# Recurrence rebuilt: 64x64 quarter tiles per head in place of zero-padded 128x128 products, and the triangular inverse by three steps from 8x8 blocks

## The chip, the cores and the metric

One core of one Trainium2 chip. The time is device microseconds of one execution of the whole program, the median of several runs; a profiled execution gives the trace. Engines: PE (matrix products, with weight loads, PEld), DVE (VectorE), ACT (ScalarE), POOL (GpSimd), SP (issues transfers).

## The reference

Two layers over 512 latent and 256 context tokens of 1024 features. Each has attention beside an RWKV-7 mixer, an output projection, and a mixture of single-neuron experts. The part that matters is the mixer's scan: 8 heads of 64 in two directions, the latent scan starting from the last context state, and the second layer needing no context output.

```python
def step(state, inp):
    r_t, w_t, k_t, v_t, kk_t, b_t = inp
    s_kk = jnp.einsum('bhij,bhj->bhi', state, kk_t)
    state = state * w_t[:, :, None, :] - s_kk[..., None] * b_t[:, :, None, :] + v_t[..., None] * k_t[:, :, None, :]
    y = jnp.einsum('bhij,bhj->bhi', state, r_t) if emit else None
    return state, y
```

## The kernel before

Per layer the program runs the projections with attention, the features of the mixer, the recurrence (`rwkv`, L692), and a tail (output projection, experts). The features leave k, b, v, r and the log decays in DRAM by chunks of 64 tokens (`FD`). `rwkv` walks 12 chunks, 4 of context and 8 latent, both directions at once. A head in a direction is one unit: 16 units of a 64x64 state. The heads are cut into two halves (`hf`); a tile of a half holds four blocks u, each with two heads, one in partitions 0 to 63 and one in 64 to 127.

To treat two heads in one product, one operand is padded: `zb` (L698) holds kh, bh, vz and zp as 128x128 blocks with zeros off the two diagonal quarters. `each` (L708) issues four products of 128x128 per half.

Five stages, each for both halves:
- A (L715): loads, exponentials of the decays (Ex, En), the scaled keys and receptances KR, and kh, bh, vz into the padded tiles (kh by POOL).
- B (L759): GB = bh by KR and GK = kh by KR, evacuated with a mask on DVE (L764, L770); kh, bh, vz transposed on PE, copied by ACT.
- C (L782): the inverse of the unit triangular 64x64 matrix in GB, begun with its 16x16 diagonal blocks: blocks gathered into D, 16 shuffles (L801) that spread their rows, 15 steps of forward substitution, two small DVE operations each (L810, L811), and X, the block diagonal (L815).
- D (L823): X grown to 32 and to 64 by two levels: a transpose (L833), q (a masked GB, by POOL through L146), two products (L839, L845), an addition to X on DVE (L846).
- E (L856): the state. zt = GK part plus H part (L860, L867), transposed to Zs (L876), Us = X by Zs (L887), the new state H by kn, bn, Vb, Us on DVE in four pieces (L897, L900, L907), the output added into zt (L919) and to Y (L928, L930).

`merge` (L136) weaves the stages: in iteration m it issues E of chunk m-2, D of m-1, B and C of m, A of m+1 and the loads of m+2, each list spread over a part of the iteration, and `outputs` (L946) of finished chunk pairs. A scheduler then orders the instructions of each engine by priority and dependence; each engine runs its own in that order. In PSUM there are four `ga` and two `ch` tiles, and one `zt` per half.

Of the kernel before, what the change touches and what calls it, by code (L numbers as in the profile page):

```python
# [21 lines left out]
D = 1024  # L22
# [15 lines left out]
def make_consts():  # L38
# [9 lines left out]
    cols["m16"] = ((p % 64)[:, None] // 16 == np.arange(4)[None])  # L48
    cols["eye16"] = (p[:, None] % 16 == np.arange(16)[None])
    cols["x16"] = (p[:, None] // 16 == np.arange(8)[None])  # L50
    P, Q = p[:, None], p[None, :]
    q1f = (P // 32 == Q // 32) & (P // 16 < Q // 16)
    q2f = (P // 64 == Q // 64) & (P // 32 < Q // 32)
    cols["q1"], cols["q2"] = q1f, q2f
# [30 lines left out]
RB = 6  # L85
# [17 lines left out]
def body(ctx: ExitStack, tc: tile.TileContext, I: dict, out: bass.AP):  # L103
# [588 lines left out]
    def rwkv(L, PT, cat, FD, need_ctx, ro, rl):  # L692
# [3 lines left out]
        rw = es.enter_context(tc.tile_pool(name=f"rw{l}", bufs=1))  # L696
# [8 lines left out]
        def bank(nm="ga", nb_=4):  # L705
            return rps.tile([128, 4, 128], F32, name=nm, bufs=nb_)

        def each(dst, f):  # L708
            for u in range(4):
                f(dst[:, u, :], u)  # L710

        def t4(nm, n=2, w=128):
            return (ra if nm in ("Ex", "En", "etot", "KR", "GB") else rw).tile([128, 4, w], F32, name=nm, bufs=n)

        def stage_a(ss):  # L715
            def load(s):
                fd = FD[s["st"], s["hf"]]
                NCH, n = TOK[s["st"]] // C, s["n"]
                fal = s["fal"] = rl.tile([128, 2, 3, 2, C], F32, name="fal", bufs=4)
                fbl = s["fbl"] = rl.tile([128, 3, 4, C], F32, name="fbl", bufs=4)  # L720
                for pp in range(2):
                    for d in range(2):
                        SP.dma_start(fal[:, d, :, pp, :],
                                     fd["a"][NCH - 1 - n if d else n, pp].rearrange("p (f t) -> p f t", t=C))
                    SP.dma_start(fbl[:, :, pp::2, :], fd["b"][n, pp].rearrange("p (f d t) -> p f d t", d=2, t=C))

            def dv(s, f, d, ps=slice(None)):
                t = s["fal"][ps, d, f]
                return t[:, :, ::-1] if d else t

            def a1(s):
                Ex = s["Ex"] = t4("Ex", 2, 65)
                En = s["En"] = t4("En", 2, 64)
                V.memset(Ex[:, :, 0:1], 1.0)
                A.activation(Ex[:, :, 1:65], s["fbl"][:, 2], AF.Exp, scale=-EXPC)
                A.activation(En, s["fbl"][:, 2], AF.Exp, scale=EXPC)
                s["etot"] = t4("etot", 8, 1)
                V.tensor_copy(s["etot"], Ex[:, :, 64:65])

            def a2(s):  # L740
                KR, Ex = t4("KR", RB), s["Ex"]
                s["KR"] = KR
                for d in range(2):
                    u = slice(2 * d, 2 * d + 2)
                    V.tensor_tensor(KR[:, u, 0:64], dv(s, 1, d), Ex[:, u, 0:64], op=mul)
                    V.tensor_tensor(KR[:, u, 64:128], dv(s, 0, d), Ex[:, u, 1:65], op=mul)

            def a3(s):
                for h in range(2):
# [3 lines left out]
                    for d in range(2):  # L753
                        A.copy(zb["vz", s["hf"]][hp, 2 * d:2 * d + 2, 64 * h:64 * h + 64], dv(s, 2, d, hp))
# [1004 lines left out]
```

## Time and profile before

| | us |
|---|---|
| median of 3 runs (4962.43 to 4966.59) | 4963.79 |
| the profiled execution, its own time | 4962.0 |
| its span on the trace | 4960.2 |
| PE busy | 4557.3 (92%) |
| DVE busy | 3918.9 (79%) |
| ACT busy | 2124.4 (43%) |
| POOL busy | 1581.4 (32%) |

The page gives means over the whole span. A stage is read by cutting the span: the recurrence of layer 0 lies near 447 to 855 us, that of layer 1 near 3186 to 3575. A product of f32 operands stands as two MATMUL records, a transpose as one. A record's duration includes a tail in the pipeline, so back-to-back records overlap, and the busy time of many by their count is their pace.

### The profile page before, as it was taken

How to read it: one execution, taken by the hardware profiler on the slowest of the kernel's cores; microseconds unless marked ns; L12 is line 12 of the kernel's file. 1: busy time of each engine (PE TensorE's matmuls, PEld its weight loads, DVE VectorE, ACT ScalarE, POOL GpSimd, SP SyncE). 2: the span in 40 equal slices, each digit the busy share in tenths (PEclk: the TensorE clock that was granted, in tenths of full speed). 3: DMA queues.
4: the chain of work that ended last, by engine and by line, in shares of the span. 5: the costliest groups of instructions: out<-in, count | busy, mean ns of one | idle time of the engine just before them, and what ended most of it. 6: DMA issues, size and time to landing. Idle time of an engine off the chain costs nothing. (4 is left out here: it accounts for less than half of the span.)

```text
span 4960.2 us, 73310 instructions
## 1 busy us (share of the span) xinstructions
PE 4557.3 (92%) x25291; PEld 3870.9 (78%) x25291; DVE 3918.9 (79%) x9256; ACT 2124.4 (43%) x3951; POOL 1581.4 (32%) x1560
## 2 busy tenths in 40 slices
PE   7998899886999999989999989889998999999999
PEld 5664898775777887767777777489877998889998
DVE  2468996699998888877788656799678986888886
ACT  3355554434775232222222235555444773333332
POOL 0212332343222345545455231333222101234441
PEclk8998999998999999999999999999999999999999
DMA  6656221644768999988899532722153768999996
GB/s 232 252 173 179 58 54 32 235 133 135 258 239 305 356 326 325 328 287 298 298 324 328 199 123 79 210 62 50 52 178 108 266 244 304 354 330 331 327 331 214
DMA packets 613733, 1105.96 MB, mean 223 GB/s; under 512 B 219056, under 2 KB 394864, under 8 KB 603632
## 3 DMA queue, kind: packets, MB, share of 16 engines
q1 hardware_dynamic: 502768, 698.57, 42.3%
q0 software_dynamic: 110592, 402.70, 22.7%
q8 instruction: 200, 3.28, 0.3%
q14 instruction: 173, 1.42, 0.1%
HBM read 960.38 MB, written 140.74 MB: 222 GB/s over the span
## 5 line engine op out<-in xcount | busy, mean ns | idle before, releaser
L1263 POOL DMA_INDIRECT u<-in_u,eidx x384 | 479.7, 1249 | 1171.8 <-DVE u L1275 833.8
L159 PE MATMUL u_ps<-phi,uhi 128*128 128x512 f32 (+1 forms) x2048 | 767.4, 375 | 62.3 <-ACT ga L1454 45.5
L159 PE MATMUL u_ps<-phi,ulo 128*128 128x512 f32 (+1 forms) x2048 | 758.9, 371 | 34.2 <-DVE ulo L1449 34.1
L159 PE MATMUL u_ps<-plo,uhi 128*128 128x512 f32 (+1 forms) x2048 | 756.1, 369 | 0.0
L1263 POOL DMA_INDIRECT u<-in_v,eidx x384 | 516.6, 1345 | 521.7 <-DVE gacc L1288 444.0
L1448 ACT CAST uhi<-raw 128x1024 fp32r<-128x1024 f32 x256 | 268.5, 1050 | 917.8 <-PE u_ps L159 574.5
L159 PE MATMUL pa<-vhi,whi 128*128 128x512 f32 x1536 | 601.1, 391 | 7.5 <-ACT whi L150 7.5
L159 PE MATMUL pa<-vhi,wlo 128*128 128x512 f32 x1536 | 603.0, 393 | 0.0
L159 PE MATMUL pa<-vlo,whi 128*128 128x512 f32 x1536 | 602.7, 392 | 0.0
L1288 DVE SCALAR_TENSOR_TENSOR gacc<-u,gw,gacc 128x1024 f32<-128x1024 f32 x381 | 488.4, 1282 | 98.3 <-DMA u<-in_v,eidx 94.7
L1275 DVE SCALAR_TENSOR_TENSOR u<-u,gh 128x1024 f32<-128x1024 f32 x384 | 468.0, 1228 | 114.8 <-DMA u<-in_u,eidx 107.3
L159 PEld LDWEIGHTS u_ps<-phi,uhi 128*128 128x128 f32 x2048 | 393.4, 192 | 117.6 <-ACT ga L1454 54.5
L159 PEld LDWEIGHTS u_ps<-phi,ulo 128*128 128x128 f32 x2048 | 392.0, 191 | 81.7 <-DVE ulo L1449 39.2
L159 PEld LDWEIGHTS u_ps<-plo,uhi 128*128 128x128 f32 x2048 | 393.2, 192 | 44.8
L1449 DVE TENSOR_TENSOR ulo<-raw,uhi 128x1024 fp32r<-128x1024 f32 x256 | 312.6, 1221 | 143.3 <-ACT uhi L1448 143.2
L150 ACT CAST whi<-w 128x512 fp32r<-128x512 f32 (+1 forms) x256 | 145.0, 567 | 619.5 <-DVE w L1596 376.6
L159 PEld LDWEIGHTS pa<-vhi,whi 128*128 128x128 f32 x1536 | 290.3, 189 | 68.1 <-issue 7.8
L159 PEld LDWEIGHTS pa<-vlo,whi 128*128 128x128 f32 x1536 | 290.4, 189 | 61.8
L159 PEld LDWEIGHTS pa<-vhi,wlo 128*128 128x128 f32 x1536 | 289.8, 189 | 61.3
L1582 DVE TENSOR_TENSOR vlo<-vraw,vhi 128x1024 fp32r<-128x1024 f32 x256 | 312.3, 1220 | 27.5 <-ACT vhi L1581 27.3
L1581 ACT CAST vhi<-vraw 128x1024 fp32r<-128x1024 f32 x256 | 263.3, 1047 | 62.6 <-PE pa L159 39.7
L1533 DVE TENSOR_SCALAR oh<-cst,gT 128x128 f32<-128x128 f32 x896 | 252.6, 348 | 0.0
(866 smaller groups left out, 9964.5 us busy)
## 6 DMA issues: line engine op xcount, KB each, us to landing
raw<-in_ut SPq DMA_DIRECT2D x256, 512.0 KB, 5.4
vraw<-in_v SPq DMA_DIRECT2D x256, 512.0 KB, 6.5
gscr<-Gs SPq DMA_DIRECT2D x28, 2048.0 KB, 8.2
mod_w<-in_mod_w SPq DMA_DIRECT2D x48, 1024.0 KB, 7.0
Gt<-gscr SPq DMA_DIRECT2D x32, 1024.0 KB, 10.4
raw<-in_w_q SPq DMA_DIRECT2D x48, 512.0 KB, 3.7
Gt<-gscr SPq DMA_DIRECT2D x32, 768.0 KB, 9.5
wo<-in_w_out SPq DMA_DIRECT2D x40, 512.0 KB, 5.0
```

Of the source, the lines that this page charges most:

```text
L150: A.copy(hi, src)
L159: PE.matmul(ps, a, b, start=first and q == 0 and j == 0, stop=last and q == n - 1 and j == 2)
L1263: G.indirect_dma_start(out=t, out_offset=None, in_=I[f"{tab}{l}"], in_offset=bass.IndirectOffsetOnAxis(ap=res["e"][:, e:e + 1], axis=0))
L1275: V.scalar_tensor_tensor(u, u, 1.0, c["h"], op0=mul, op1=mul, accum_out=c["act"][:, e:e + 1])
L1288: V.scalar_tensor_tensor(acc, v, w[:, e:e + 1], acc, op0=mul, op1=add)
L1448: A.copy(uhi, ut)
L1449: ins = V.tensor_tensor(ulo, ut, uhi.bitcast(F32), op=sub)
L1533: V.tensor_scalar(o2[:, t, :], io, T3[:, 1, t0 + t:t0 + t + 1], T3[:, 2, t0 + t:t0 + t + 1], op0=ALU.is_equal, op1=mul)
L1581: A.copy(r["vhi"], vt)
L1582: gafter(V.tensor_tensor(r["vlo"], vt, r["vhi"].bitcast(F32), op=sub), f)
```

## The change

`rwkv` is rewritten. Chunks are no longer cut into halves: one tile [128, 2 s, 4 g, 64] carries all units, head r in partitions 64r to 64r + 63. No padded tile is left. Products are 64x64 by 64 or 128 columns. `cross` issues 16 of them (four g, four pairs r, s), reading partitions of half r, writing those of half s, in the order (0,0), (1,1), (0,1), (1,0); `along` issues 16 that read and write the same half. A work tile `wk` [128, 2, 512] in PSUM has a slice of 512 for each r, and there are three of them; `zy` has one buffer.

The inverse starts from 8x8 blocks (seven shuffles, seven substitution steps), and three rounds W <- W (2I - AW) grow it: W transposed (d0), AW (d1), S = 2I - AW on DVE, W S (d2), copied by ACT. d3 then applies the inverse to bn and to GB's r half once (XB), so that the state stage needs Zs and XB alone: Zs comes out of `zy` without a transpose, and Us is gone. `settle` is a tiny ACT read of a PSUM tile between `cross` and `along` into it. Where a chunk's output isn't needed (context of layer 1) the r half is left out. kh and the masks of q move off POOL: kh is made by DVE, q is gone.

```diff
+    cols["mp"] = 0.5 * mf[:, :64]
+    cols["n8"] = -0.5 * ((s // 8 == t // 8) & (t < s))
+    cols["eye"] = (s == t)
+    cols["eye2"] = 2.0 * (s == t)
+    cols["eye8"] = (p[:, None] % 8 == np.arange(8)[None])
+    cols["x8"] = ((p[:, None] % 64) // 8 == np.arange(8)[None])
...
-        zb = {}
-        for nme in ("kh", "bh", "vz", "zp"):
-            for hf in range(2):
-                t = ra.tile([128, 4, 128], F32, name=f"{nme}{hf}")
-                G.memset(t, 0.0)
-                zb[nme, hf] = t
...
+        BOTH = ((0, 0), (1, 1), (0, 1), (1, 0))
+
+        def work():
+            return rps.tile([128, 2, 512], F32, name="wk", bufs=3)
...
+        def cross(dst, lh, rh, lo=0, first=None):
+            for g in range(4):
+                for r, s in BOTH:
+                    hp = slice(64 * r, 64 * r + 64)
+                    PE.matmul(dst[64 * s:64 * s + 64, r, g, :], lh[hp, s, g, :], rh[hp, s, g, :],
+                              start=True if first is None else first and g == 0, stop=True,
+                              skip_group_check=first is not None)
+
+        def settle(t):
+            A.copy(ra.tile([128, 2, 4, 1], F32, name="settle", bufs=2), t[:, :, :, 0:1])
+
+        def along(*sets):
+            for dst, lh, rh in sets:
+                for part in (BOTH[:2], BOTH[2:]):
+                    for g in range(4):
+                        for r, s in part:
+                            hp = slice(64 * r, 64 * r + 64)
+                            PE.matmul(dst[hp, s, g, :], lh[hp, s, g, :], rh[hp, s, g, :], start=False, stop=True,
+                                      skip_group_check=True)
+
+        def flips(tp, src):
+            src = flat(src)
+            for g in range(4):
+                PE.transpose(tp[:, 128 * g:128 * g + 128],
+                             src[:, 2 * g:2 * g + 2, :].rearrange("p s n -> p (s n)"), ident)
...
+            def b0():
+                gt = quad(work(), 64)
+                cross(gt, s["KR"][:, :, :, 0:64], s["bh"])
+                dm = s["dm"] = t8("dm", 1)
+                V.tensor_tensor(dm, gt, bc(K("n8")), op=mul)
+
+            def b1():
+                gb = quad(work(), w)
+                cross(gb, s["bh"], s["KR"][:, :, :, :w])
+                s["AT"] = t8("AT", 3)
+                BG = s["BG"] = t8("BG", 3, 128)
+                V.tensor_tensor(s["AT"], gb[:, :, :, 0:64], bc(K("mp")), op=mul)
+                if s["emit"]:
+                    V.tensor_tensor(BG[:, :, :, 64:128], gb[:, :, :, 64:128], bc(K("n")[:, 64:128]), op=mul)
+                V.tensor_tensor(s["AT"], s["AT"], bc(K("eye")), op=add)
...
+            def b3():
+                t = work()
+                flips(t[:, 0, :], s["kh"])
+                flips(t[:, 1, :], s["bh"])
+                s["kn"] = t8("kn", 3)
+                unflip(s["kn"], t[:, 0, :])
+                unflip(s["BG"][:, :, :, 0:64], t[:, 1, :], -0.5)
...
+            def c0():
+                w["D"] = ra.tile([128, 8, 8], F32, name="D8", bufs=2)
+                V.tensor_reduce(w["D"], flat(s["dm"]).rearrange("p x (b j) -> p x j b", j=8), axis=AX.X, op=add)
...
+                if q0 == 1:
+                    w["N"] = ra.tile([128, 8, 8, 8], F32, name="Nb")
+                for q in range(q0, min(8, q0 + 4)):
+                    V.stream_shuffle(w["N"][:, q], w["D"], [(x // 8) * 8 + q for x in range(32)])
...
+                V.tensor_tensor(tm[:, :, :q], X8[:, :, q:q + 1].to_broadcast([128, 8, q]), Nb[:, q, :, :q], op=mul)
+                V.tensor_tensor(X8[:, :, :q], X8[:, :, :q], tm[:, :, :q], op=add)
+
+            def c4():
+                W = s["W"] = t8("W", 4)
+                V.tensor_tensor(flat(W).rearrange("p x (b t) -> p x b t", t=8),
+                                w["X"][:, :, None, :].to_broadcast([128, 8, 8, 8]),
+                                K("x8")[:, None, :, None].to_broadcast([128, 8, 8, 8]), op=mul)
+
+            return [c0, lambda: c2(1), lambda: c2(5)] + [lambda q=q: c3(q) for q in range(7, 0, -1)] + [c4]
...
+        def stage_d(s):
+            def d0():
+                t = work()
+                flips(t[:, 0, :], s["W"])
+                s["WT"] = t8("WT", 2)
+                unflip(s["WT"], t[:, 0, :])
+
+            def d1():
+                t = quad(work(), 64)
+                cross(t, s["AT"], s["W"])
+                s["S"] = t8("S", 2)
+                V.tensor_tensor(s["S"], bc(K("eye2")), t, op=sub)
+
+            def d2():
+                t = quad(work(), 64)
+                cross(t, s["WT"], s["S"])
+                s["W"] = t8("W", 4)
+                A.copy(s["W"], t)
+
+            def d3():
+                w = 128 if s["emit"] else 64
+                t = quad(work(), w)
+                cross(t, s["W"], s["BG"][:, :, :, :w])
+                s["XB"] = t8("XB", 2, 128)
+                A.copy(s["XB"][:, :, :, :w], t)
+
+            return [d0, d1, d2] * 3 + [d3]
...
+        def stage_e(s):
+            def e0():
+                zy = s["zy"] = rps.tile([128, 2, 4, 128], F32, name="zy", bufs=1)
+                if s["emit"]:
+                    cross(zy[:, :, :, 64:128], s["Vb"], s["GK"][:, :, :, 64:128], first=True)
+                cross(zy[:, :, :, 0:64], s["GK"][:, :, :, 0:64], s["Vb"], first=not s["emit"])
+                if H[0] is not None:
+                    settle(zy[:, :, :, 0:64])
+
+            def e1():
+                zy, h, KR = s["zy"], H[0], s["KR"]
                 if h is not None:
...
+                    sets = [(zy[:, :, :, 0:64], KR[:, :, :, 0:64], h)]
+                    if s["emit"]:
+                        sets.append((zy[:, :, :, 64:128], h, KR[:, :, :, 64:128]))
+                    along(*sets)
+                s["Zs"] = t8("Zs", 2)
+                A.copy(s["Zs"], zy[:, :, :, 0:64])
+
+            def e2():
+                if s["more"]:
+                    s["hq"] = quad(work(), 64)
+                    cross(s["hq"], s["kn"], s["Vb"], first=True)
+                    settle(s["hq"])
+
+            def e4():
...
+                    along((hq, s["XB"][:, :, :, 0:64], s["Zs"]))
+                    et = s["etot"].to_broadcast([128, 2, 4, 64])
+                    hn = t8("H", 3)
                     if h is None:
-                        V.tensor_scalar(hn[:, u, :], hq[:, u, :], s["etot"][:, u, :], None, op0=mul)
+                        V.tensor_tensor(hn, hq, et, op=mul)
                     else:
-                        V.scalar_tensor_tensor(hn[:, u, :], hq[:, u, :], s["etot"][:, u, :], s["He"][:, u, :],
-                                               op0=mul, op1=add)
-                H[s["hf"]] = hn
...
+                        V.tensor_tensor(hn, hq, h, op=add)
+                        V.tensor_tensor(hn, hn, et, op=mul)
+                    H[0] = hn
+
...
+                along((zy[:, :, :, 64:128], s["Zs"], s["XB"][:, :, :, 64:128]))
...
-        SS = [[dict(st=st, n=n, hf=hf, more=not (st == "l" and n == NL // C - 1)) for hf in range(2)]
+        SS = [dict(st=st, n=n, more=not (st == "l" and n == NL // C - 1), emit=st == "l" or need_ctx)
...
             if m >= 2:
-                todo.append((0.0, 1.0, stage_e(SS[m - 2])))
+                todo.append((0.0, 0.8, stage_e(SS[m - 2])))
...
                 todo.append((0.0, 0.4, stage_b(SS[m])))
-                todo.append((0.25, 1.0, stage_c(SS[m])))
+                todo.append((0.15, 1.0, stage_c(SS[m])))
```

The order of DVE's instructions in a steady latent iteration of layer 1, around the end of stage C and the state update. Before (X, X_32110 the inverse; H the state; D, Nb the blocks and their spread rows):

```order
L810 TENSOR_TENSOR xtm<-X_32110,Nb 128x8
L811 TENSOR_TENSOR X_32110<-X_32110,xtm 128x8
L815 TENSOR_TENSOR X<-X_32110,cst 128x512
L907 SCALAR_TENSOR_TENSOR H<-ch,etot,He 128x128 x4
L815 TENSOR_TENSOR X<-X_32110,cst 128x512
L738 COPY etot<-Ex 128x4
L806 COPY X_32884<-cst 128x128
L907 SCALAR_TENSOR_TENSOR H<-ch,etot,He 128x128 x4
L738 COPY etot<-Ex 128x4
L846 TENSOR_TENSOR X<-ga,X 128x512 x2
L764 TENSOR_TENSOR GB<-ga,cst 128x512
L789 TENSOR_SCALAR D_32408<-GB,cst 128x64
```

After the change, in the same place:

```order
L873 TENSOR_TENSOR S<-cst,wk 128x2x4x64
L928 TENSOR_TENSOR H<-wk,H 128x2x4x64
L929 TENSOR_TENSOR H<-H,etot 128x2x4x64
L771 COPY etot<-Ex 128x2x4
L873 TENSOR_TENSOR S<-cst,wk 128x2x4x64
L856 TENSOR_TENSOR W<-X_31564,cst 128x512
L848 COPY X_32417<-cst 128x64
L797 TENSOR_TENSOR dm<-wk,cst 128x2x4x64
L837 TENSOR_REDUCE D_31864<-dm 128x64
L843 STREAM_SHUFFLE Nb<-D_31864 128x64 x7
```

The two halves' operations, which stood side by side, have become one operation on all units. Between the second and the third S stand only the state update and etot, and between the third S and dm only W and a copy.

The order of PE's products in the same iteration, around the end of stage D. Before (two halves in turn; operands are named moving, then stationary):

```order
L919 MATMUL zt_32322<-GB,Us 128x128 x4
L845 MATMUL ga<-X,R 128x128 x4
L919 MATMUL zt_32355<-GB,Us 128x128 x4
L845 MATMUL ga<-X,R 128x128 x4
L762 MATMUL ga<-KR,bh_29019 128x128 x4
L860 MATMUL zt_32709<-GK,Vb 128x128 x4
L762 MATMUL ga<-KR,bh_29021 128x128 x4
L768 MATMUL ga<-KR,kh_29015 128x128 x4
```

After the change:

```order
L736 MATMUL wk<-cst,W 128x128 x4
L717 MATMUL wk<-W,AT 64x64 x16
L717 MATMUL zy<-GK,Vb 64x64 x13
L717 MATMUL wk<-S,WT 64x64 x16
L717 MATMUL zy<-GK,Vb 64x64 x3
L717 MATMUL zy<-Vb,GK 64x64 x8
L717 MATMUL wk<-BG,W 64x128 x16
L717 MATMUL wk<-bh,KR 64x64 x16
L736 MATMUL wk<-cst,W 128x128 x4
L717 MATMUL zy<-Vb,GK 64x64 x8
L717 MATMUL wk<-KR,bh 64x128 x16
```

These are the third round (flips of W, d1, d2), d3 (BG, W), b0 of the next chunk (bh, KR), and the first flips of the next chunk's W; b0, from which DVE makes dm, now stands behind d3, and full-array transposes stand between quarter tiles.

## Rows read from the trace of the kernel before

**Rows 1.** The page: the span and the busy time of engines.

```profile
span 4960.2 us, 73310 instructions
...
PE 4557.3 (92%) x25291; PEld 3870.9 (78%) x25291; DVE 3918.9 (79%) x9256; ACT 2124.4 (43%) x3951; POOL 1581.4 (32%) x1560
```

**Rows 2.** Busy time by stretch, recurrence: from:to, length, engines (instructions), granted clock, DMA share, GB/s.

```profile
462.60:512.40 49.80, 33.88 (x241) 31.94 (x242) 45.30 (x192) 20.79 (x51) 17.65 (x24) 0.83 0.43 100
512.40:809.60 297.20, 275.43 (x2397) 270.52 (x2396) 275.08 (x1074) 160.61 (x403) 96.72 (x120) 0.99 0.19 43
809.60:854.90 45.30, 42.23 (x349) 40.65 (x348) 17.64 (x48) 14.51 (x29) 7.23 (x6) 0.96 0.06 13
3197.10:3247.80 50.70, 35.67 (x239) 34.44 (x240) 47.08 (x202) 21.41 (x54) 18.23 (x24) 0.80 0.63 146
3247.80:3530.00 282.20, 259.71 (x2276) 255.52 (x2275) 267.05 (x1061) 157.05 (x392) 91.05 (x116) 0.99 0.18 41
3530.00:3575.30 45.30, 42.11 (x348) 40.54 (x347) 17.73 (x47) 14.51 (x29) 7.24 (x6) 0.96 0.05 12
sum 770.50, PE 689.01 PEld 673.61 DVE 669.88 ACT 388.89 POOL 238.12; mean PE 114.84 PEld 112.27 DVE 111.65 ACT 64.81 POOL 39.69
```

**Rows 3.** The same for three steady iterations, all engines (PE, PEld, DVE, ACT, POOL); L764 alone.

```profile
695.30:781.00 85.70, 80.93 (x722) 80.28 (x722) 81.96 (x321) 49.06 (x127) 27.94 (x36) 1.00 0.09 20
...
512.40:809.60 297.20, 13.71 (x20) 0.99 0.19 43
...
695.30:781.00 85.70, 4.13 (x6) 1.00 0.09 20
```

**Rows 4.** Groups by line, 695.3 to 781: count | busy us, mean ns | idle before.

```profile
L801 DVE STREAM_SHUFFLE Nb<-D 128x128 f32<-128x128 f32 x48 | 10.7, 297 | 0.1
...
L752 DVE TENSOR_TENSOR bh<-fbl,En 64x256 f32<-64x256 f32 x12 | 5.0, 415 | 0.2
...
L764 DVE TENSOR_TENSOR GB<-ga,cst 128x512 f32<-128x512 f32 x6 | 4.1, 689 | 0.1
```

**Rows 5.** Groups by form, DVE, 695.3 to 781: substitution steps by size.

```profile
L811 DVE TENSOR_TENSOR X<-X,xtm 128x56 f32<-128x56 f32 x3 | 0.7, 219 | 0.1
...
L811 DVE TENSOR_TENSOR X<-X,xtm 128x16 f32<-128x16 f32 x3 | 0.5, 176 | 0.1
```

**Rows 6.** Operations by tile and line, whole span: duration ns min/median/max, first and last start, forms.

```profile
L153 DVE TENSOR_TENSOR wolo<-wo,wohi x40: 1214/1220/1227, 865.8 to 3633.2; 128x1024 fp32r<-128x1024 f32 x40
...
L430 DVE TENSOR_REDUCE ass<-at x12: 279/808/822, 126.0 to 2997.4; 128x10 f32<-128x640 f32 x10, 128x2 f32<-128x128 f32 x2
```

**Rows 7.** PE in order of time (start us, length us), and a group by form, 447 to 860.

```profile
202.68 0.28 PE L159 MATMUL pr_ps<-hlo,wrhi 128*128 128x256 f32 x1
202.80 0.28 PE L159 MATMUL pr_ps<-hhi,wrlo 128*128 128x256 f32 x1
203.01 1.07 PE L195 MATMUL mod_ps<-mod_w,cs 128*32 128x512 f32 x8
204.01 0.50 PE L159 MATMUL pr_ps<-hhi,wrhi 128*128 128x512 f32 x1
204.34 0.39 PE L159 MATMUL pr_ps<-hlo,wrhi 128*128 128x512 f32 x1
...
308.71 1.93 PE L534 MATMUL a_po<-PTs,vv 128*64 128x512 f32 x6
...
L994 PE MATMUL ga<-sgdl,gup 128*128 128x64 f32 x48 | 5.9, 274 | 0.0
```

**Rows 8.** All engines in order of time, 619.5 to 626: a transpose and the copy that waits for it.

```profile
620.81 0.60 PE L833 MATMUL ga<-cst,X 128*128 128x128 f32 x4
...
621.50 0.59 ACT L835 COPY XT<-ga 128x512 f32<-128x512 f32 x1
```

More of the change, by code (lines that the diff above doesn't have):

```diff
@@ L708, in each @@
[L708 to L717, printed above, removed]
-                NCH, n = TOK[s["st"]] // C, s["n"]
[L719 to L735, printed above, removed]
-                A.activation(En, s["fbl"][:, 2], AF.Exp, scale=EXPC)
[L737 to L742, printed above, removed]
-                for d in range(2):
[L744 to L749, printed above, removed]
-                    hp = slice(64 * h, 64 * h + 64)
-                    gmul(zb["kh", s["hf"]][hp, :, 64 * h:64 * h + 64], s["fbl"][hp, 0], s["En"][hp])
-                    V.tensor_tensor(zb["bh", s["hf"]][hp, :, 64 * h:64 * h + 64], s["fbl"][hp, 1], s["En"][hp], op=mul)
-                    for d in range(2):
-                        A.copy(zb["vz", s["hf"]][hp, 2 * d:2 * d + 2, 64 * h:64 * h + 64], dv(s, 2, d, hp))
-            return [[lambda s=s: load(s) for s in ss],
-                    [lambda s=s, f=f: f(s) for f in (a1, a2, a3) for s in ss]]
@@ new lines, in work, with quad, bank, t8 @@
+        def work():
+            return rps.tile([128, 2, 512], F32, name="wk", bufs=3)
+        def quad(t, n):
+            return t[:, :, :4 * n].rearrange("p s (g n) -> p s g n", n=n)
+        def bank():
+            return work()[:, 0, :].rearrange("p (a b) -> p a b", b=128)
+        def t8(nm, n, w=64):
+            return ra.tile([128, 4, 2, w], F32, name=nm, bufs=n).rearrange("p g s n -> p s g n")
+        def flat(t):
+            return t.rearrange("p s g n -> p g s n").rearrange("p g s n -> p (g s) n")
@@ new lines, in stage_b, with b2, b4 @@
+        def stage_b(s):
+            w = 128 if s["emit"] else 64
[13 more added lines that the diff above has]
+                V.tensor_tensor(s["AT"], s["AT"], bc(K("eye")), op=add)
+            def b2():
+                gk = quad(work(), w)
+                cross(gk, s["kh"], s["KR"][:, :, :, :w])
+                s["GK"] = t8("GK", 3, 128)
+                V.tensor_tensor(s["GK"][:, :, :, :w], gk,
+                                K("m")[:, None, None, :w].to_broadcast([128, 2, 4, w]), op=mul)
+            def b3():
[5 more added lines that the diff above has]
+                unflip(s["BG"][:, :, :, 0:64], t[:, 1, :], -0.5)
+            def b4():
+                t = work()
+                flips(t[:, 0, :], s["vz"])
+                s["Vb"] = t8("Vb", 3)
+                unflip(s["Vb"], t[:, 0, :])
+            return [b0, b1, b2, b3, b4]
@@ L913, in e5 @@
+                        V.tensor_tensor(hn, hn, et, op=mul)
+                    H[0] = hn
+            def e5():
+                st, n, zy = s["st"], s["n"], s["zy"]
                 NCH = TOK[st] // C
-                if st == "c" and not need_ctx:
+                if not s["emit"]:
                     return
@@ L930, in e5 @@
                         V.tensor_tensor(yv, src, yv, op=add)
-            return [lambda s=s, f=f: f(s) for f in (e0, e1, e2, e3, e4, e5) for s in ss]
+            return [e0, e1, e2, e4, e5]
         sg = {}
@@ L1003, in rwkv @@
         items = [("c", n) for n in range(NCX // C)] + [("l", n) for n in range(NL // C)]
[L1004 removed]
+        SS = [dict(st=st, n=n, more=not (st == "l" and n == NL // C - 1), emit=st == "l" or need_ctx)
               for st, n in items]
[L1006 removed]
+        AA = [stage_a(s) for s in SS]
         NI = len(items)
```

195 lines of the change are left out of this document (56 added, 139 removed).

## The prediction

> **What bounds the kernel now.** I read the page first, then the busy time by stretch, then the groups of instructions of one steady stretch, and last the order of time around a few single steps. The page [rows 1] shows PE and DVE as the two busy engines, but as means over stages. The change touches one stage, the recurrence, so the table by stretch decides [rows 2]. Per layer I cut it at starts of the GB evacuations (L764): fill (m = 0 and 1), ten full iterations (m = 2 to 11), drain (m = 12 and 13). The fills take 49.8 and 50.7 us, the twenty full iterations 297.2 + 282.2 = 579.4 (29.0 each), the drains twice 45.3: 770.5 us in all, 15.5% of the span.
>
> In three iterations without output work [rows 3] six GB evacuations, two per iteration, take 85.7 us, so an iteration is 28.6 us. In it DVE is busy 81.96 us (27.3 per iteration, 96%) and PE 80.93 (27.0, 94%). So both bound it, and a change must relieve both. ACT has 16.4 and POOL 9.3 us per iteration.
>
> The sum is made against the profiled execution, 4962.0 us beside a span of 4960.2; the median of the runs is 1.8 us above it. A measurement tells 0.2% (10 us) from no change.
>
> **PE, part by part.** Now an iteration issues 96 padded products, two MATMUL records each, and 48 transposes of one record: 240 records, and 722 records in three iterations were busy 80.93 us, 0.112 us apiece [rows 3].
>
> After, a chunk has 13 calls of `cross` and 4 of `along`, each 16 products, so 32 records: 544, plus 24 transposes. Ten crosses stream 64 columns, three (b1, b2, d3) 128. A 128-column record costs 0.112; I put a 64-column one at half, 0.056. The row against it is the gate product L994, 64 columns at 5.9/48 = 0.123 [rows 7], but there a 128-wide weight load stands before each, and here the load is 64 wide.
>
> What decides is whether the array's quarters work at once. For column tiles the trace shows it: eight records of L195, four 32-wide tiles by two passes of 512 columns, take 1.07 us together, and six of L534 on two 64-wide tiles 1.93 us [rows 7]; a full record of 512 columns in turn would need 4 x 0.112 = 0.45 us, so 3.6 and 2.7. For row tiles the trace shows nothing: every product has 128 rows. So I bound it:
> - all four quarters at once: 8 records per quarter and cross: 10 x 8 x 0.056 = 4.5, 3 x 8 x 0.112 = 2.7; `along` uses only the two diagonal quarters: 4 x 16 x 0.056 = 3.6; transposes 24 x 0.11 = 2.6 (four take 0.60 with the tail [rows 8]); 13.4 us.
> - only columns at once: the crosses and alongs double: 9.0 + 5.4 + 7.2 + 2.6 = 24.2 us.
> - none at once: 17.9 + 10.8 + 7.2 + 2.6 = 38.5 us.
>
> Changing between full array and tiles costs too: L195 begins 0.21 us after the record before it, where these follow each other by 0.12, and the first full record after it takes 0.50 instead of 0.39 [rows 7]. That is 0.1 us per change; six changes per iteration (the PE excerpt of the change has three) give 0.6, and I put 1 us. [...]
>
> I take the first case, 14.4 us, because column tiles do what the code says and nothing in the rows sets rows apart from columns: `cross` gives each row half its own PSUM half (index r) as L195 gives each tile its own partitions.
>
> **DVE, part by part.** Gone are the four D products per half, 16 shuffles of 128x128 (0.297 [rows 4]), 30 substitution steps, four X additions (L846), eight narrow H updates and the zp copies. After, per iteration:
> - twelve 128x512 operations (dm, AT, BG, AT+eye, three S, W, kh, bh, two for H) at 0.689 as GB [rows 4]: 8.3;
> - one 128x1024 (GK) at 1.22 [rows 6]; one reduction over 128x512, from 0.808 for 128x640 [rows 6]: 0.7;
> - four KR products of 256 elements at 0.415, as bh now [rows 4]: 1.7; the Y additions, two of 256 in half the chunks: 0.4;
> - seven shuffles of 128x64: between 0.297 at twice the size and 0.18 for the smallest operations; I take 0.23: 1.6;
> - fourteen substitution steps from 128x56 (0.219) down to 128x8, 0.176 at 128x16 [rows 5]: 2.7; small copies 0.4.
>
> That is 17.0 us against 27.3. kh moves from POOL to DVE and is counted; POOL loses q, kh and the zeroing, and nobody waits for it any more. SP issues the same 12 loads per chunk. ACT: 15 operations near 0.6 us each and the 1024-wide XB at 1.0, with two tiny `settle` reads: about 10 us, covered.
>
> **The new waits.** Before, two halves ran as two chains, and while one waited the other worked. Now one chain carries all heads: d1, S on DVE, d2, copy of W on ACT, three times. Two places leave DVE idle, by the DVE excerpt of the change. A hop between engines costs 0.1 us (PE ends at 621.41, ACT starts at 621.50 [rows 8]).
> - From the second to the third S: hop, d2 0.45 + 0.27 tail, hop, copy 0.58, hop, flips 0.45, d1 0.7, hop: 2.85 us. DVE has the two H operations and etot in it, 1.6. Idle 1.25.
> - From the third S to dm: hop, d2 0.7, hop, copy 0.58, hop, d3 0.9, b0 0.7, hop: 3.28 us, since d3 stands ahead of b0, dm's product, on PE. DVE has W and a copy, 0.9. Idle 2.38.
>
> With these 3.6 us and the 4% that DVE idles now (0.8), an iteration is 17.0 + 3.6 + 0.8 = **21.4 us**, longer than PE's 14.4 and ACT's 10.
>
> **The sum.** Twenty iterations at 21.4 are 428; output steps (DVE 3.2 us, partly in the idle places) add 2 in four of them, 8; layer 1's context chunks leave out the r half, 2 us in three iterations, -6: 430 for 579.4, so 149 less. The fills, where DVE was busy 45.3 and 47.1 us [rows 2], shrink by 17.0/27.3 to 58, with the idle places 74 for 100.5: 26 less. The drains are now bound by PE (42 of 45.3); after, one chain of three rounds (9.2 by the hops above) and d3 is 11.4, and an output chain runs beside it; I put 16 per iteration, 64 for 90.6: 27 less. Together 202: 4962.0 - 202 = **4760 us**. The tail and the features are not touched and follow as before.
>
> **Rivals.** That the products don't become quarter tiles is none: the order of the change shows them as 64x64 and 64x128.
> - Rows take turns, only columns overlap: PE 25.2/0.95 = 26.5 us per iteration becomes the bound. Twenty are 532 with the same corrections, 47 less; fill and drain 21 less: **4894**. For: no row here has fewer than 128 rows. Against: the four L195 tiles share every row and do not disturb each other.
> - **Slower: the small records don't overlap**, because quarters that alternate row and column record by record are taken in turn. PE then needs 39.5 us per iteration, at 0.95 busy 41.6: 20 x (41.6 - 29.0) = 252 and 10 more in the fills: **5225**. It decides from 27.3 us of PE per iteration, that is 48 ns per record (568 records). For: 0.123 us for L994's 64 columns. Against: L195 and L534. [...]
> - The waits do not appear, because the three wk buffers let PE run ahead: 17.8 us per iteration, 20 x 3.6 = 72 less and some more in the fill: about **4680**.
> - PE, with idle places of its own, is granted less clock. In the fills, busy 68%, it had 0.83 and 0.80, in full iterations 0.99 [rows 2]. At 0.83, 13.4 us become 16, still under DVE, and d1, d2, d3 lengthen the two idle places by under 1 us: 4780, inside the main case. At half clock throughout PE needs 28 us: no change.
>
> **How the numbers follow.** The main case (4690 to 4830, for the shuffles, the waits and the clock) 75%; rows in turn 10%; slower 9%; the rest 6%, half of it half clock or a wait that eats the gain, 3%, a point each to slower and two to faster. So faster 0.87, same 0.03, slower 0.10. The range 4690 to 4900 takes in the main case and rows in turn; left out are slower and same, 13%, and some 5% below 4690.
>
> **What would show it.** Right: 64*64 records of PE at some 0.45 us for 32 of a cross plus the tail, DVE near 17 us busy per iteration with idle time before S and dm that PE and ACT end, iterations of 21 to 22 us, POOL almost idle. Wrong: 32 records of a 64-column cross over 0.9 us (rows in turn) or over 1.7 (all in turn); PE busy and DVE idle through an iteration; S or dm waiting for a free wk buffer; a granted clock under 0.8 in the full iterations.

## The result, and the profile after

The changed kernel takes 4804.31 us, median of 4 runs (4792.44 to 4804.97); the kernel before took 4963.11 in the runs beside it. The ratio is 0.9673 (95%: 0.9656 to 0.969), 159 us less. The profiled execution took 4804.7 us for 4962.0, 157 less, where the sum had 202.

The page, for [rows 1]:

```profile
span 4802.9 us, 85326 instructions
...
PE 4308.1 (90%) x32715; PEld 3589.6 (75%) x32715; DVE 3620.7 (75%) x7842; ACT 1942.4 (40%) x3407; POOL 1353.9 (28%) x1256
```

PE has 249 us less work and DVE 298, and the time falls by 157: more waits than before. The busy time by stretch of the changed kernel, cut as [rows 2] (end of the attention, dm (L797) of chunk 2, end of the state of chunk 9, last addition to Y; columns as there):

```profile
462.50:508.00 45.50, 21.61 (x549) 19.15 (x550) 32.10 (x120) 15.83 (x33) 0.00 (x0) 0.77 0.64 160
508.00:744.80 236.80, 180.75 (x5468) 160.36 (x5467) 149.75 (x485) 85.01 (x174) 7.45 (x5) 0.92 0.19 49
744.80:780.20 35.40, 31.21 (x824) 27.21 (x822) 14.48 (x35) 10.32 (x19) 5.93 (x5) 0.99 0.11 27
3121.55:3165.70 44.15, 22.98 (x549) 20.20 (x550) 27.41 (x109) 16.73 (x34) 0.00 (x0) 0.65 0.76 194
3165.70:3384.60 218.90, 161.09 (x5060) 142.91 (x5061) 140.02 (x464) 78.60 (x166) 1.64 (x1) 0.88 0.21 58
3384.60:3419.90 35.30, 31.11 (x817) 27.18 (x818) 14.37 (x35) 10.31 (x19) 6.02 (x5) 0.97 0.11 24
```

| | before | forecast | after |
|---|---|---|---|
| two fills | 100.5 | 74 | 89.7 |
| twenty iterations | 579.4 | 430 | 455.7 |
| two drains | 90.6 | 64 | 70.7 |
| sum | 770.5 | 568 | 616.1 |

So 154 of the 157 us are the recurrence's. The twenty iterations are of two kinds, with loads and without; the latter are called late below. Four in a row, cut at dm, same columns:

```profile
616.80:644.00 27.20, 22.18 (x588) 19.46 (x588) 17.98 (x58) 10.49 (x22) 2.91 (x2) 0.94 0.29 76
644.00:671.00 27.00, 19.47 (x597) 17.36 (x597) 15.26 (x50) 9.00 (x20) 0.00 (x0) 0.87 0.28 75
671.00:690.50 19.50, 16.44 (x569) 14.68 (x569) 14.99 (x49) 8.04 (x18) 0.00 (x0) 1.00 0.01 3
690.50:709.80 19.30, 16.38 (x569) 14.68 (x570) 14.82 (x47) 7.65 (x18) 0.00 (x0) 1.00 0.02 5
```

DVE's work is alike in the last three, yet one takes 27.0 us and two 19.4. The DMA share tells them apart: after the last load of a layer (chunk 11, issued at 656) an iteration takes 19.4 us, 2 under the forecast; with loads it takes 27.2 on average in layer 0 (508 to 671, six in 163 us) and 24.2 in layer 1, where context chunks have no r half (3165.7 to 3310.8, six in 145). The trace in order of time, in the iteration from 644, shows what a load does there (start, length, idle before and its releaser):

```profile
655.49 0.69 DVE L783 TENSOR_TENSOR bh<-fbl,En 128x512 f32<-128x512 f32 x1
656.21 2.51 SPq L757 DMA_DIRECT2D fbl<-fdb0l  x4
656.83 0.69 PE L717 MATMUL wk<-S,WT 64*64 64x64 f32 x32
658.81 5.64 SPq L755 DMA_DIRECT2D fal<-fda0l  x8
662.19 0.64 ACT L768 ACTIVATE Ex<-fbl 128x512 f32<-128x512 f32 x1 [6.44 <-DMA fbl<-fdb0l]
662.73 0.61 ACT L769 ACTIVATE En<-fbl 128x512 f32<-128x512 f32 x1
663.25 0.56 ACT L879 COPY W<-wk 128x512 f32<-128x512 f32 x1
663.87 1.12 PE L736 MATMUL wk<-cst,W 128*128 128x128 f32 x4 [5.31 <-ACT W L879]
664.91 1.13 PE L717 MATMUL wk<-W,AT 64*64 64x64 f32 x32
666.11 0.69 DVE L873 TENSOR_TENSOR S<-cst,wk 128x512 f32<-128x512 f32 x1 [6.64 <-PE wk L717]
```

bh frees the buffer of fbl at 656.2, and only then does SP issue the next load into it, that of chunk 11. The exponential Ex of that chunk, which is not needed before its KR at 699.5, stands next on ACT and waits for the load, 6.44 us. Behind it stands the copy of W, whose product (S, WT) had ended at 657.5: the chain of rounds waits with it, PE for 5.31 us and DVE for 6.64. Then the clock adds its part. By stretch, for PE before, in and after its idle time:

```profile
654.00:658.60 4.60, 4.11 (x161) 3.69 (x160) 3.44 (x9) 1.75 (x6) 0.00 (x0) 1.00 0.22 58
658.60:663.80 5.20, 0.00 (x0) 0.00 (x0) 0.84 (x2) 1.61 (x4) 0.00 (x0) 0.94 0.77 197
663.80:668.70 4.90, 4.76 (x116) 4.11 (x116) 1.48 (x3) 1.72 (x5) 0.00 (x0) 0.50 0.30 67
```

PE comes back from 5.31 us of idle time at a granted clock of 0.50, and d1 (W, AT) takes 1.13 us where it takes 0.64 at 1.00. Over the whole span, the idle time before Ex by releaser (us, times):

```profile
L768 ACT ACTIVATE Ex<-fbl x24: 618/634/639, 465.6 to 3302.6; 128x512 f32<-128x512 f32 x24
...
  DMA fbl<-fdb0l: 39.5, 7
  DMA fbl<-fdb1l: 39.4, 6
  DMA sgdc<-PT: 10.7, 1
  DMA fbl<-fdb0c: 10.0, 2
...
  DMA fbl<-fdb1c: 4.7, 2
```

That is 93.6 us of waits for fbl in 17 of 24 exponentials. Before the change it was 16.8 us, in 4 of 48 (an Ex was half a chunk then):

```profile
L735 ACT ACTIVATE Ex<-fbl x48: 400/416/437, 445.4 to 3460.3; 128x256 f32<-128x256 f32 x48
...
  DMA fbl<-fdb1c: 9.0, 1
  DMA fbl<-fdb0c: 5.6, 2
  DMA fbl<-fdb0l: 2.2, 1
```

The change itself let Ex run so far ahead. Its two buffers held the two halves of one chunk and now hold two whole chunks, while those of the loads hold two chunks as before. Before, the loads into fbl for chunk 11 of layer 0 were issued from 710.7 to 718.0, and its two exponentials ran at 738.9 and 740.0; now the load is issued at 656.2, and Ex runs at 662.2, when it lands.

In a late iteration, without them, the forecast's own waits can be read (DVE in order of time, the operations that waited):

```profile
690.49 0.69 DVE L797 TENSOR_TENSOR dm<-wk,cst 128x512 f32<-128x512 f32 x1 [2.44 <-PE wk L717]
703.99 0.69 DVE L928 TENSOR_TENSOR H<-wk,H 128x512 f32<-128x512 f32 x1 [1.08 <-PE wk L730]
706.05 0.69 DVE L873 TENSOR_TENSOR S<-cst,wk 128x512 f32<-128x512 f32 x1 [0.64 <-PE wk L717]
709.83 0.69 DVE L797 TENSOR_TENSOR dm<-wk,cst 128x512 f32<-128x512 f32 x1 [2.26 <-PE wk L717]
```

Two operations of the same iteration that follow each other without a wait:

```profile
695.29 0.68 DVE L807 TENSOR_TENSOR AT<-AT,cst 128x512 f32<-128x512 f32 x1
695.89 0.68 DVE L873 TENSOR_TENSOR S<-cst,wk 128x512 f32<-128x512 f32 x1
```

The records of a cross, d2, in PE's order of time:

```profile
702.96 0.69 PE L717 MATMUL wk<-S,WT 64*64 64x64 f32 x32 [0.78 <-DVE S L873]
```

### The profile page after: what moved, and what is told of

Read it like the earlier page. It is cut to its first block, busy times and chain, and to the rows that moved or that the text cites. A ratio compares the mean times of both kernels' runs of the same rounds, so it can differ in the third digit from the quotient of the medians.

```text
span 4802.9 us, 85326 instructions
## 1 busy us (share of the span) xinstructions
PE 4308.1 (90%) x32715; PEld 3589.6 (75%) x32715; DVE 3620.7 (75%) x7842; ACT 1942.4 (40%) x3407; POOL 1353.9 (28%) x1256
## 3 DMA queue, kind: packets, MB, share of 16 engines
q14 instruction: 151, 1.24, 0.1%
## 5 line engine op out<-in xcount | busy, mean ns | idle before, releaser
L1601 DVE TENSOR_TENSOR vlo<-vraw,vhi 128x1024 fp32r<-128x1024 f32 x256 | 312.2, 1220 | 25.8 <-ACT vhi L1600 25.7
```

The lines of the kernel that those rows point to most:

```text
L1601: gafter(V.tensor_tensor(r["vlo"], vt, r["vhi"].bitcast(F32), op=sub), f)
```

## The experiments

Every kernel below is the changed kernel with the edit shown. Times are medians of 4 runs if nothing else is said. What lies outside the recurrence, which none of them edits, took 4169 to 4191 us in the profiled executions; so a difference of up to some 20 us in the whole time need not be the recurrence's. Kernels are therefore also compared by the recurrence alone, from the last copy of the attention (ao) to the last addition to Y, both layers, in the profiled execution: 771.9 us before, 616.8 after.

**One exponential ahead.**

```diff
-                Ex = s["Ex"] = t8("Ex", 2, 65)
-                En = s["En"] = t8("En", 2)
+                Ex = s["Ex"] = t8("Ex", 1, 65)
+                En = s["En"] = t8("En", 1)
```

> Ex and En get one buffer instead of two, so that the exponentials of a chunk cannot stand on ACT two chunks ahead; the loads stay as they are. Theory (ACT's queue: in the changed kernel Ex stands ahead of the copy of W, and waits for its load, 93.6 us in 17 waits, while iterations with such a wait take 26 to 27 us and those after the last load 19.4): the waits of Ex on the load fall under 20 us, the iterations with loads come down to 20 to 22 us, and the time is 4720 to 4750. Rival (the loads themselves are too slow, 12 transfers of 0.62 us of issue each per chunk behind a buffer that comes free late): the wait only moves to KR on DVE, and the time stays at 4795 to 4810. Second rival (the granted clock of 0.87 in these iterations, 1.00 in the late ones, is the cause and not the effect): with the waits gone the clock would still be under 0.9 and the iterations over 24 us, 4770 to 4800.

Measured: 4757.05 us (ratio to before 0.9585, 0.9566 to 0.9604), 47 less than the changed kernel, with the loads' buffers as they were. The recurrence took 574.3 us. In layer 0 the first iteration took 19.1 us, the others with loads 22.5 to 23.6, but for two of 27 to 28 with output steps; in layer 1 they took 16.6 to 23.2. Ex's idle time:

```profile
  DVE KR L779: 23.5, 8
...
  DMA fbl<-fdb0c: 9.6, 2
  DMA fbl<-fdb1l: 9.6, 4
...
  DMA fbl<-fdb1c: 4.6, 2
  DMA fbl<-fdb0l: 2.9, 1
```

The waits for fbl fell from 93.6 to 26.7 us, where under 20 was expected, and the time is 7 us above its range; part of the reason may be that Ex now waits on ACT for KR, which frees its only buffer, 23.5 us in 8 places. With one buffer Ex stands one chunk ahead, as it did before the change. The first rival, slow loads, falls. The second, the clock, falls as the main cause: it rose to 0.92 or 0.93 in three of the four iterations of 22.5 to 23.6 us when the waits went (0.85 in the other).

**A third buffer.** The third lies in the recurrence's own pool, the other two where they were.

```diff
+                k3 = (n + (0 if s["st"] == "c" else NCX // C)) % 3
+                pool, nb = (ra, 1) if k3 == 2 else (rl, 2)
-                fal = s["fal"] = rl.tile([128, 3, 2, 4, C], F32, name="fal", bufs=2)
-                fbl = s["fbl"] = rl.tile([128, 3, 2, 4, C], F32, name="fbl", bufs=2)
+                fal = s["fal"] = pool.tile([128, 3, 2, 4, C], F32, name="fal", bufs=nb)
+                fbl = s["fbl"] = pool.tile([128, 3, 2, 4, C], F32, name="fbl", bufs=nb)
```

> fal and fbl get a third buffer, so that a chunk's loads need not wait for bh and vz of the chunk two before; Ex keeps its two buffers and its place ahead of the copy of W on ACT. Theory (what ACT's Ex waits for is a load that is issued only when bh has freed its buffer, some 5 us before): the loads are issued most of an iteration earlier, the waits of Ex on a load fall from 93.6 us to under 20, the iterations with loads come to 20 to 22 us, and the time is 4720 to 4755, as with one exponential ahead (4757) or below it. Rival (the queue is the limit: 12 issues of 0.62 us each per chunk, and transfers of small packets): the waits stay over 60 us and the time is 4785 to 4810.

Measured: 4761.71 us (0.96, 0.9584 to 0.9617), recurrence 571.0. Ex waits 29.6 us for fbl, and 20.0 for KR. The waits and the time both miss their ranges, the time by 7 us. By another way it gives nearly the same, 43 us less, so ACT's queue behind a late load is shown twice. That the two edits end at the same limit, an Ex too early on ACT, is likely by the 50 us of waits that either leaves, but no run shows it.

**Two quarters at a time.**

```diff
-            for g in range(4):
-                for r, s in BOTH:
+            for r in range(2):
+                for g, s in [(g, s) for g in range(4) for s in range(2)]:
```

> cross issues all products that read the lower 64 partitions first and then all that read the upper ones, so that two quarters of the array, not four, have work at a time; the products are the same. Theory (all four quarters of the array work at once, so 32 records of a 64-column cross take 0.69 us): now two work at once, the 32 records take 1.1 to 1.2 us, 13 crosses take 7.2 us more per iteration, some 4 us of it on the chain of the late iterations (19.4 to 23 or 24 us), and the time is 4860 to 4910. Rival (records start at a fixed rate of some 14 ns whichever quarter they use): 0.69 us still, and 4795 to 4810.

Measured: 4853.81 us (one run), recurrence 663.9. The same d2 in a late iteration, and that iteration's busy time by stretch:

```profile
717.73 0.98 PE L717 MATMUL wk<-S,WT 64*64 64x64 f32 x32 [0.22 <-DVE S L873]
```

```profile
711.60:732.10 20.50, 19.40 (x569) 17.89 (x570) 14.84 (x48) 8.00 (x18) 0.00 (x0) 1.00 0.02 4
```

The same 32 records take 0.98 us for 0.69, and PE is busy 19.4 of 20.5 us, for 16.4 of 19.3. The order of the quarters counts, so they do work at once, and a fixed rate of issue falls. The sizes were missed: the late iteration takes 20.5 us where 23 to 24 was expected, and the time is 6 us under its range. The cross takes less than the 1.1 to 1.2 expected because the upper half's records begin some 0.3 us after the first, while the lower half's still run.

**b0 ahead of d3.**

```diff
-            return [d0, d1, d2] * 3 + [d3]
+            return [d0, d1, d2] * 3, [d3]
...
             if m >= 2:
                 todo.append((0.0, 0.8, stage_e(SS[m - 2])))
+                todo.append((0.05, 0.06, DD[m - 2][1]))
             if 1 <= m <= NI:
-                todo.append((0.02, 1.0, stage_d(SS[m - 1])))
+                DD[m - 1] = stage_d(SS[m - 1])
+                todo.append((0.02, 0.95, DD[m - 1][0]))
```

> d3 of a chunk is issued at the start of the next iteration, behind b0, so that PE makes dm's product before it applies the inverse. Theory (in the late iterations DVE idles 2.3 us before dm, since d3's 0.9 us stand ahead of b0): the idle time before dm falls to some 1.3 us, the late iterations go from 19.4 to 18.5, and the time falls by 5 us (if ACT's wait for the load swallows it in the other iterations) to 20 us (if it counts in all): 4784 to 4799. Rival (XB, which d3 makes, is late for the state, so what dm gains H loses): 4800 to 4810.

Measured: 4785.36 us (0.9639, 0.9623 to 0.9655), 19 less; recurrence 607.9, only 9 less. The other 10 us lie in stages that the edit doesn't touch.

```profile
681.68 0.69 DVE L797 TENSOR_TENSOR dm<-wk,cst 128x512 f32<-128x512 f32 x1 [0.55 <-PE wk L717]
```

dm waits 0.55 us here and 1.9 in two late iterations together, for 2.44 and 2.26. Only 0.3 us of that is kept in such an iteration (19.1), as S waits longer (3.3 us in the two for 1.1), which points to the chain of rounds. Up to the last dm the recurrence gets 16 us shorter, and its drains, from there to the last addition to Y, 7 us longer.

**kh on POOL.**

```diff
-                V.tensor_tensor(s["kh"], s["fbl"][:, 0], s["En"], op=mul)
+                G.tensor_tensor(s["kh"], s["fbl"][:, 0], s["En"], op=mul)
```

> kh goes back to POOL, one operation of 128x512 per chunk. Theory (the late iterations of 19.4 us are bound by the chain of the three rounds, in which DVE idles 4 us, and the earlier ones by ACT's wait): DVE loses 0.6 us of busy time per iteration, but the time stays within 6 us of 4804. Rival (DVE bounds the iteration): 0.6 us in twenty-two iterations are 13 us less, 4788 to 4793. A second rival: POOL is slower at it than DVE and b2 then waits for kh, 4810 to 4830.

Measured: 4798.22 us (0.9665, 0.9644 to 0.9687), recurrence 612.3, the late iterations of layer 0 19.7 and 19.8. The time is as expected, but the test is not what it was meant to be, for DVE got no less busy: 30.6 us in two late iterations for 29.8. While POOL makes kh, until 677.77, the DVE operation beside it, with two inputs in SBUF, lasts until 677.81:

```profile
676.49 1.28 POOL L784 TENSOR_TENSOR kh<-fbl,En 128x512 f32<-128x512 f32 x1 [24.75 <-ACT W L879]
```

```profile
676.57 1.24 DVE L851 TENSOR_TENSOR xtm<-X,Nb 128x32 f32<-128x32 f32 x1
```

The same xtm takes 0.18 us in the changed kernel. So whether DVE's busy time bounds the late iterations stays open here.

**ysq on POOL.**

```diff
-                A.copy(w["sq"].rearrange("p i (h c) -> p i h c", c=64), nr[:, :, :, None].to_broadcast([128, 4, 2, 64]))
+                G.tensor_copy(w["sq"].rearrange("p i (h c) -> p i h c", c=64), nr[:, :, :, None].to_broadcast([128, 4, 2, 64]))
```

> The broadcast of the output's reciprocal deviations (ysq from nr) moves from ACT, where it stands ahead of copies of Vb and WT and waits 28.1 us in ten places for POOL's power, to POOL itself, behind that power. Theory (an in-order wait on ACT costs the chain of rounds its length): the two output iterations of layer 0 go from 27.3 us to 24 or 25, the output steps in the drains lose a little, and the time falls by 5 to 12 us, 4792 to 4799. Rival (the wait is covered by the wait for the load that follows it on ACT): 4800 to 4808. Second rival: POOL is slower at the copy than ACT (0.62 us) and the transposes behind it on PE wait, 4805 to 4815.

Measured: 4801.12 us (0.9679, 0.9662 to 0.9695), recurrence 617.7: no change, by the first rival's number. But it is no change only in sum. The two drains, in which no Ex is left, fell by 3.5 us each (to 48.7, from the last dm to the last addition to Y). The two output iterations went from 27.5 and 27.2 to 30.1 and 32.6 us; in the first of them Ex waits 5.2 us for fbl, where the wait of ysq, 4.7 us, stood before. Why the second grew more is open.

**16x16 base blocks, two rounds.**

```diff
-            return [d0, d1, d2] * 3 + [d3]
+            return [d0, d1, d2] * 2 + [d3]
...
-                for q in range(q0, min(8, q0 + 4)):
+                for q in range(q0, min(16, q0 + 4)):
...
-            return [c0, lambda: c2(1), lambda: c2(5)] + [lambda q=q: c3(q) for q in range(7, 0, -1)] + [c4]
+            return [c0] + [lambda q=q: c2(q) for q in (1, 5, 9, 13)] + [lambda q=q: c3(q) for q in range(15, 0, -1)] + [c4]
```

> The base blocks are 16x16 again: 15 shuffles of 128x128 and 15 substitution steps on DVE, and two rounds of W (2I - AW) instead of three; all else as in the changed kernel. Theory (the iterations without loads are bound by the chain of the rounds with DVE idle 4 us in it; one round is some 4.5 us of the chain, but DVE takes 2 us more of shuffles and 3.7 us more of steps, less one S of 0.6): DVE busy goes from 15 to 20 us per iteration and bounds it, the late iterations go from 19.4 to 21 or 22, the earlier ones stay near 27, as ACT's wait is the same: 4800 to 4830. Rival (the chain is all that counts): late iterations of 15 to 17 us, 4740 to 4790.

Measured: 4786.59 us (0.9645, 0.9629 to 0.9661), recurrence 595.6, faster than with 8x8 blocks and outside the theory's range. The time lies in the rival's range, but the late iterations behave as the theory said, not in the rival's 15 to 17 us:

```profile
672.20:693.90 21.70, 15.95 (x513) 14.60 (x512) 19.73 (x78) 6.73 (x16) 0.00 (x0) 0.90 0.01 3
```

DVE is busy 19.7 of 21.7 us. But most of the earlier ones came to 18 to 22 us, where 27 was expected (25.8 and 27.3 with output steps): Ex's waits for fbl were 39.9 us. Why they fell is not shown. So the 8x8 blocks alone win 2.3 us in a late iteration, and lose some 5 us in one with loads.

**The edits together.** Third buffer, b0 ahead of d3 and ysq on POOL:

> The third buffer, b0 ahead of d3 (4785 alone), and ysq on POOL together. Theory (separate waits on one chain, so they add): third buffer -50 to -80, b0 ahead of d3 -15 to -20, ysq -5 to -12, so 4695 to 4735, and iterations of 18.5 to 20 us with a granted clock over 0.95. Rival (another engine or DVE's 15 to 17 us of work comes next): no more than the third buffer alone, within 5 us of it.

Measured: 4736.12 us (0.9548, 0.9532 to 0.9564), recurrence 551.7. By the whole times they add: 43, 19 and 3 apart, 68 together. The recurrence says it better: 46, 9 and -1 apart, but 65 together, so one of them gains in company what it doesn't alone; the next run tells which. An iteration with loads and one with output steps:

```profile
528.10:548.40 20.30, 16.23 (x568) 14.59 (x568) 15.50 (x49) 8.85 (x20) 0.00 (x0) 1.00 0.33 83
593.20:617.40 24.20, 20.92 (x598) 17.97 (x598) 18.11 (x58) 9.51 (x21) 3.52 (x3) 1.00 0.33 82
```

The clock is 1.00 in these two, where it was 0.87 and 0.94 in the same places. In layer 1 it is still 0.84 to 1.00 in the iterations with loads, and Ex still waits 16.2 us for fbl there, the fill included.

Without ysq on POOL:

> The third buffer and b0 ahead of d3, without moving ysq to POOL: what of the 4736 of the three together is ysq's. If the three add (ysq alone took nothing that can be told from zero, 4801 for 4804, but there the wait for the load stood behind it), this is 4736 to 4742 and the two output iterations of layer 0 are 24 us as with ysq on POOL. If ysq counts once the waits for loads are gone, these two stay at 27 us, and the time is 4742 to 4750.

Measured: 4743.51 us, but from 4727.4 to 4755.49, which does not decide; recurrence 563.1, output iterations 25.2 and 26.4. That is 54 us under the changed kernel's recurrence, about the 46 and 9 of the two edits apart. The 11 us that ysq adds in the profile lie where output steps are: 3.3 in the two output iterations, 8.2 in the drains. By the times it isn't shown.

With 16x16 blocks:

> 16x16 base blocks and two rounds, together with the third buffer, b0 ahead of d3 and ysq on POOL. Theory (with 16x16 blocks DVE has some 20 us of work per iteration and bounds it at 21 to 22 us, and it was faster than 8x8 alone, 4787 for 4804, only since fewer copies on ACT stand behind the waiting Ex): with the waits gone the 8x8 blocks win, this is 4760 to 4785 beside 4736, and its iterations are 21 to 22 us. Rival (the shorter chain is the gain, and DVE's extra work fits into its idle time): 4715 to 4736, iterations under 20 us.

Measured: 4761.3 us (0.9601, 0.9585 to 0.9617), recurrence 572.3, iterations of layer 0 mostly 21.2 to 21.5. With most of the waits gone 8x8 blocks and three rounds are 25 us faster, 21 in the recurrence.

With kh on POOL:

> kh on POOL together with the third buffer, b0 ahead of d3 and ysq on POOL. With the waits gone DVE is busy 15.4 of some 19.5 us. Theory (the iteration is still a chain through PE, ACT and DVE, and what stands on DVE between two links of it counts): between a few tenths of a microsecond less per iteration and nothing, 4726 to 4738. Rival (DVE bounds it by its order): 0.6 us in 22 iterations, 4720 to 4726. Second rival: POOL is late with kh, which b2 and the flips of kh wait for: 4740 to 4760.

Measured: 4735.15 us (0.9547, 0.9531 to 0.9563), recurrence 559.0: iterations of 22.3 to 22.7 us with loads for 20.3 to 20.6; no gain. POOL takes 1.27 to 1.78 us for kh where DVE takes 0.69, and beside it a KR product on DVE takes 1.5 us for 0.42.

**Two pools again.** The kernel before had one more thing that the change took away, and the forecast passed over: its first tiles lay in a small SBUF pool, the rest in a second.

```diff
+        rw = es.enter_context(tc.tile_pool(name=f"rw{l}", bufs=1))
...
-            return ra.tile([128, 4, 2, w], F32, name=nm, bufs=n).rearrange("p g s n -> p s g n")
+            pool = ra if nm in ("Ex", "En", "etot", "KR", "kh", "bh", "vz", "dm") else rw
+            return pool.tile([128, 4, 2, w], F32, name=nm, bufs=n).rearrange("p g s n -> p s g n")
```

> The third buffer, b0 ahead of d3 and ysq on POOL, and the recurrence's tiles in two SBUF pools again, as before the change: Ex, En, etot, KR, kh, bh, vz and dm in a small one, the rest in another. In the changed kernel, with one pool for all, the recurrence's first operation (Ex of chunk 0) starts at 465.6 us in layer 0, when the last transfer out of the attention (ao, issued at 462.5) has landed; before, with two pools, it started at 445.4, beside the attention. Theory (the first tile of a pool waits until all the memory under that pool is free, so the small pool lets stage A of the first chunks run beside the attention): Ex of chunk 0 starts 10 to 20 us earlier, dm of chunk 0 5 to 7 us earlier (463.8 before), since its PSUM comes free with the attention's end, and the time falls by 8 to 16 us over two layers, 4720 to 4728 beside 4736. Rival (the loads of chunk 2, or the products' PSUM, hold the fill anyway): Ex starts earlier, dm of chunk 2 does not, and the time stays at 4732 to 4740.

Measured: 4728.86 us, 5 runs (4710.99 to 4732.29; ratio 0.9524, 0.9509 to 0.954), recurrence 540.5 for 551.7 (the three edits together). The first exponentials before the change, in the changed kernel, and with two pools again:

```profile
445.36 0.42 ACT L735 ACTIVATE Ex<-fbl 128x256 f32<-128x256 f32 x1
```

```profile
465.57 0.63 ACT L768 ACTIVATE Ex<-fbl 128x512 f32<-128x512 f32 x1 [10.71 <-DMA sgdc<-PT]
```

```profile
445.73 0.64 ACT L772 ACTIVATE Ex<-fbl 128x512 f32<-128x512 f32 x1
```

In the changed kernel the trace puts the end of the wait down to sgdc, a load that Ex doesn't read and that was issued 0.4 us behind the last ao transfer; in layer 1, and in both layers of five other runs, it names that transfer (cat_l<-ao, 9.9 us). With two pools Ex starts 20 us earlier, dm of chunk 0 at 463.4 for 471.0, dm of chunk 2 at 502.7 for 508.6 (the three edits together): 7.4 us less in layer 0's recurrence and 3.7 in layer 1's. The traces of the run with two pools show no such wait; the two intervals of the whole time still touch. This is the fastest kernel here.

## Why the prediction was right or wrong

The direction and the range held, and so did the mechanism of the gain, quarters of the array that work at once and less work for DVE; of 202 us 157 came.

- **PE, right.** Four quarters work at once. A cross of 64 columns takes 0.69 us with the tail, forecast 0.72; its records start in groups of four, 7 ns apart in a group and 58 ns from group to group, forecast 56. PE is busy 16.4 us per late iteration, against 14.4; how much of the 2 us are tails, and how much changes between full array and quarters, is not told apart. The 32 records start within 0.48 us, 15 ns apiece. The rivals of rows in turn and of records that do not overlap fall.
- **DVE's work, oversized.** 14.9 us per late iteration for 17.0. Durations of the rows were added where operations overlap: 128x512 operations start 0.60 us apart though each lasts 0.68, shuffles 0.14 apart though each lasts 0.22. One term was too small: the reduction, put at 0.7, lasts 1.11.
- **The two waits, nearly right.** Before dm 2.3 to 2.4 us, forecast 2.38; from the second to the third S 1.08 + 0.64, forecast 1.25. The 1.08 stand before H, which waits for the state's products, not for the round; the forecast didn't name that wait. Late iterations take 19.4, forecast 21.4: the 2 us are DVE's work.
- **Where the sum failed: "ACT ... covered" and "SP issues the same 12 loads per chunk".** Loads and exponentials were costed by their durations and held to be hidden. Before, Ex hardly waited for loads into fbl, 16.8 us in all; now its buffers reach one chunk further ahead, and it stands on ACT for a load that has only just been issued, ahead of the copy of W, on which the one chain of all heads depends: 93.6 us. Giving Ex its old reach, or the loads a buffer more, took 64 to 67 us of these waits away and 43 to 47 us of the time. That one chain in place of two also makes each wait dearer is plausible, but no run tests it. Iterations with loads took 24 and 27 us on average in the two layers, all twelve some 50 us over their part of the forecast, while the other eight were some 25 us under it. So the total came this near by luck: without the oversized DVE work, 2 us in each of twenty iterations, the forecast would have been some 40 us lower, and nearly twice as far off. This is the rival "a wait that eats the gain" in part, which had a chance but no price.
- **Fills, 11 of 26 us.** The forecast scaled DVE's work, and left out that one pool in place of two makes the first tile wait until 465.6: two pools gave back 11, beside the three edits. In the fill too Ex waits for loads, 3.2, 6.8 and 6.4 us in layer 0.
- **Drains, 20 of 27 us.** 35.4 each for 32, a tenth more. Whether the chain bounds them, as the forecast had it, is not shown: PE is busy 31.2 of 35.4 us.
- **The clock** was granted at 0.79 to 0.94 in iterations with loads, and at 1.00 in the late ones. The forecast's sign of being wrong, under 0.8, shows in one of the twenty (0.79). It followed ACT's wait, as the third buffer with its company shows (1.00 in most of layer 0's), and adds to its price: 7.6 us for a wait of 6.4.

## What to carry to other kernels

When two half-sized chains become one, look on every engine for what stands ahead of the chain's links and waits for something slow, and price that wait in full: there may be no second chain beside it. An operation that is early in a queue is not free, if what it waits for is late (here 93.6 us in 17 waits); a buffer more, or one less for the early operation, moves it (here 64 and 67 us of them). Where tiles grow, count buffers in units of work, not in tiles: the same number of larger tiles lets an operation run further ahead. Where a change merges pools of tiles, ask when the first tile gets its memory (here Ex started at 465.6 us with one pool and at 445.7 with two).

## What the runs showed of the hardware

- Products on four 64x64 quarters of the array started 7 ns apart in groups of four, and 32 records of 64 columns took 0.69 us; in the order with the lower half's records first the same 32 took 0.98.
- After 5.3 us without products TensorE came back at a granted clock of 0.50, and the stretch of 4.9 us from there ran at it: a wait on ACT of 6.4 us cost an iteration 7.6 (27.0 for 19.4).
- Two 128x512 operations of DVE that don't depend on each other overlapped: they started 0.60 us apart, and each lasted 0.68.
- While POOL made kh, a 128x512 product (1.27 to 1.28 us), a DVE operation with two inputs in SBUF took 1.15 to 1.24 us in place of about 0.2, in eight iterations; the xtm of 128x32 took 1.24 for 0.18.
